# w_out's first 512 channels by Strassen's seven products, with sums taken in the accumulator banks

## The chip, the cores and the metric

The kernel runs on one core of a Trainium2 chip. Its time is the device time of one execution in microseconds (us). The engines named are TensorE (PE; PEld is its weight load), VectorE (DVE), ScalarE (ACT), GpSimd (POOL) and SyncE (SP, which issues the loads of weights).

## The reference

A decoder layer in float32 on 256 tokens with 1024 channels: a half-weighted SwiGLU layer, two parallel mixers (a Mamba-2 scan and differential attention), whose results are merged by gates and projected, and a second half-weighted SwiGLU layer, each inside RMS norms. What matters here is the middle of it:

```python
gates = jax.nn.sigmoid(gate_logits + gate_b[l]).reshape(b, L, N_BRANCH, D_MODEL)
merged = gates[:, :, 0] * y_ssd + gates[:, :, 1] * y_att
h = h + rmsnorm(merged @ w_out[l], mix_post_g[l])
h = h + 0.5 * rmsnorm(swiglu(rmsnorm(h, ffn2_pre_g[l]), ffn2_w_gate[l], ffn2_w_up[l], ffn2_w_down[l]),
                      ffn2_post_g[l])
```

`merged` is 256x1024, `w_out` 1024x1024.

## The kernel before

**Precision.** Every large product is done in three terms. A float32 operand is split into a high part (a cast on ScalarE, line 259 for weights) and a low part (raw minus high on VectorE, line 260); the terms are high x high, low x high and high x low. One matmul takes a slice of 128 channels, 128 tokens and 512 columns. So w_out takes 8 slices x 2 token blocks x 2 column halves x 3 terms = 96 matmuls.

**Weights.** SyncE loads chunks of 1 MB into three buffers (`raw`). `take` hands out the next unit of weights and, with `split_to`, has units split ahead of their use: each unit takes two casts `whi` and two subtractions `wlo` of 128x1024. A chunk's buffer is loaded anew (`load_to`) as soon as its last reader is done. A chunk of w_out is 256 channels by 1024 columns.

**Order.** TensorE's instructions run in the order in which the code writes them (`own_order(PE)`); those of VectorE, ScalarE and SyncE are put in order by a scheduler from that point of the program on. On the chip each engine does its own in the order that was set.

**The stretch around the change.** `natural` computes, for a half of the 512 columns at a time, the gates' products (`pgt`), the scan's projection (`pws`) and the attention's projection (`pwd`), for two token blocks each. When `pwd` of column half q is done, `merge` multiplies and adds with the gates (lines 1613 and 1614, tiles `gt`), and `turn_merged` turns the half by transposes on TensorE (`pmg`) and splits it into `mh` and `ml` (lines 320 and 321), so that channels stand on partitions. Both blocks of half 0 are turned after the first unit of `pwd` of half 1; half 1 is turned in w_out's first two slices. Then `mm_n` (line 676) does w_out into four banks `acc_mx`, one for each token block and column half. It does block 0's two banks first, then block 1's.

**What follows block by block.** `norm_half` takes the sum of squares of a bank on ScalarE (`jp_mxp`, line 506) and multiplies the bank by the gain on VectorE (`og_mxp`, line 605). `norm_end` has GpSimd make the reciprocal root in two steps (`rp_mxp`, lines 511 and 512), and VectorE adds the product to the residual `h` (line 645, one for each half). For the next norm, block 0 is turned raw (`pu_f`, line 520, during the last matmuls of w_out) and scaled later; its gained parts are `u_f` (lines 526 and 528). Block 1 is scaled first: two squares of `h` on ScalarE (`sq_f`), two steps on GpSimd (`r_f`), `un_f` on VectorE (line 565), and only then its turn `pu_f`, which TensorE's order has after 36 matmuls `pn_f` of the feed-forward layer's first product on block 0.

**Products by sevens that exist already.** The down projections of both feed-forward layers do part of their channels by Strassen's scheme in Winograd's form. A `Quad` is two chunks (512 channels) as four quarters of 256 channels by 512 columns. Three products take a quarter as it is (1, 2 and 3), four take a sum of quarters (5, 6, 7 and 4; `sum_of`, line 122, tile `wt`). `split` (lines 130 and 136) makes high and low part of each, `wqh` and `wql`. `sums_of` (lines 737 to 740) makes the four sums of the activations, `sv`, and splits them.

Of the kernel before, what the change touches and what calls it, by code (L numbers as in the profile page):

```python
# [47 lines left out]
SSD_US = 1.55  # L48
DOWN = {"f1": "q1 p q2 p q3 ppp", "f2": "q1 p q2 p q3 ppp"}
FIRST, LAST = (1, 2, 3, 5, 7, 6, 4), (1, 6, 7, 2, 3, 5, 4)  # L50
BREAK, STOP = object(), object()


@with_exitstack
def tile_hybrid_layer(ctx: ExitStack, tc: tile.TileContext, x, ffn1_pre_g, ffn1_w_gate, ffn1_w_up,
# [37 lines left out]
    class Quad:  # L93
# [60 lines left out]
    def n_chunk(w, k0):  # L154
        chunk(w[k0:k0 + 2 * P, :].rearrange("(j p) c -> p j c", p=P), [P, 2, D])

    def quad(w, k0, products):

        n = len(units)
        for k in (k0, k0 + 2 * P):  # L160
            n_chunk(w, k)
        del units[n:]
        q = Quad(len(chunks) - 2, products)
        units.extend((q, p) for p in products)


# [427 lines left out]

    def norm_half(n, b, q, acc, pg, fold, tag, cs=slice(0, 512)):

        if q == 0:
# [7 lines left out]
        n["mul"] = nc.vector.tensor_tensor(n["og", q][:, cs], acc[:, cs], pg[:, halves[q]][:, cs], ALU.mult).ins  # L605
# [124 lines left out]
    def sums_of(g, even, odd):  # L730
# [11 lines left out]
        split(more[:, 0], more[:, 1], v[:, 3])  # L742
        return ([hi[:, i] for i in range(3)] + [more[:, 0]], [lo[:, i] for i in range(3)] + [more[:, 1]])

    def mm_quads(acts, sums, tag):


# [10 lines left out]
        for n, (kind, j) in enumerate(of_quads):  # L758
            last = n == n_quads - 1
            if kind == "p":  # L760
                wh, wl = take()
                for kt in range(2):
                    ah, al = acts[2 * j + kt]
                    for b in range(2):
                        ts = slice(b * P, (b + 1) * P)
                        for x_, w_ in ((ah, wh), (al, wh), (ah, wl)):
                            for q in range(2):
                                p = ((2, 3), (4, 8))[b][q]
                                mm(p, x_[:, ts], w_(kt)[:, halves[q]], False)
                continue  # L770
            sh, sl = sums[j]
            for p in LAST if last else FIRST:
                wh, wl = take()
                for kt in range(2):
                    if p in (1, 2, 4):
                        k, b = {1: (0, 0), 2: (2, 0), 4: (2, 1)}[p]
                        ah, al = (x_[:, b * P:(b + 1) * P] for x_ in acts[4 * j + k + kt])
                    else:
                        ah, al = (x_[{5: 0, 6: 1, 7: 2, 3: 3}[p]][:, kt, :] for x_ in (sh, sl))
# [762 lines left out]

    own_order(PE)

    def natural(name, n, hi, lo, evict, us, then=lambda: None):


        accs = [pj(f"{name}{b}") for b in range(2)]
        for i in range(n):
            w = take()  # L1550
            for b in range(2):
                bs = slice(b * P, (b + 1) * P)
                mm_nat(accs[b], w, (lambda k: hi(k)[:, bs], lambda k: lo(k)[:, bs]), i * 4, i == 0, i == n - 1, "u")
# [14 lines left out]
    for half in range(2):  # L1568
        gb = k4([P, D], f"gb{half}")
        nc.gpsimd.dma_start(gb, gate_b[0][half * D:(half + 1) * D].partition_broadcast(P))  # L1570
        for b in range(2):
            gt[half][b] = k4([P, D], f"gt{half}{b}")
        for q in range(2):
            def gate(b, acc):
                nc.vector.tensor_tensor(gt[half][b][:, halves[q]], acc, gb[:, halves[q]], ALU.add)

            natural(f"pgt{half}{q}", 2, uh, ul, gate, GATE_US)
    opens.append(open_gates)
# [1 line left out]
        back.run(0.1)  # L1580
    for q in range(2):
        def gated(b, acc):
            t = gt[0][b][:, halves[q]]
# [6 lines left out]
    mg, merges = [], []  # L1590

    def turn_merged(n):

        for q, b, t, mh, ml in merges[:n]:
            pt = bg([P, 4, P], f"pmg{q}{b}")
            for m in range(4):
                nc.tensor.transpose(pt[:, m, :], t[:, m * P:(m + 1) * P], ident)
            bs = slice(b * P, (b + 1) * P)
            split(mh[:, :, bs], ml[:, :, bs], pt)
        del merges[:n]  # L1600

    def attended():
        back.drain()
        act_table(SILU)

    for q in range(2):
        mh = k4([P, 4, T], f"mh{q}", F32R)
        ml = k4([P, 4, T], f"ml{q}", F32R)
        mg += [(mh[:, m, :], ml[:, m, :]) for m in range(4)]

        def merge(b, acc):
            t0, t1 = gt[0][b][:, halves[q]], gt[1][b][:, halves[q]]
            nc.vector.tensor_tensor(t1, acc, t1, ALU.mult)
            nc.vector.tensor_tensor(t1, t1, t0, ALU.add)
            merges.append((q, b, t1, mh, ml))

        natural(f"pwd{q}", 2, lambda j: oh[j // 4][:, j % 4, :], lambda j: ol[j // 4][:, j % 4, :], merge,
                SSD_US if q == 0 else 0.0, (attended, lambda: turn_merged(2))[q])

    pg = load_gain(mix_post_g, "pg_mx")  # L1620
    acc = [[bg([P, 512], f"acc_mx{b}{q}") for q in range(2)] for b in range(2)]

    made, ready, turned = next_norm("f2", "f2")

    def mixed(b):
        n = {}
        for q in range(2):
            norm_half(n, b, q, acc[b][q], pg, 1.0, "mxp")
        norm_end(n, b, 1.0, "mxp")
        ready(b)  # L1630

    mm_n(acc, mg, mixed, turned, lambda: turn_merged(1))


    norm = made[0]
# [36 lines left out]
```

## Time and profile before

| | |
|---|---|
| median of 3 runs | 730.2 us (729.93 to 730.43) |
| the profiled execution's own time | 730.82 us |
| its span, first to last instruction | 728.9 us |
| granted TensorE clock over the span | 0.998 |
| issues of loads of w_out, 1 MB each | 4, 5.0 us to landing |
| POOL busy in the span | 30.6 us |

The busy time of an engine is the time in which one of its instructions runs; "idle before" and "<-" name how long an engine stood idle and what ended that. In a timeline each row has its start and its length in us from the span's start, and xN counts equal instructions that follow each other. A matmul's row is longer than the distance to the next, since matmuls overlap.

### The profile page before, as it was taken

To read this page: it belongs to the slowest core of one execution; us is meant where nothing else is said; L and a number is where in the kernel's file an instruction comes from. 1 tells how busy PE (TensorE), PEld (TensorE's weight loads), DVE (VectorE), ACT (ScalarE), POOL (GpSimd) and SP (SyncE) were. 2 spreads that over 40 slices of the span, in tenths; PEclk is the share of its full clock that TensorE was granted. 3 is DMA by queue.
4 is the path that set the end of the run, shared out by engine and by line. 5 is a ranking of instruction groups with operands and counts; after the bars stand their busy time and mean duration, and the time that the engine had idled before them with its cause. 6 is when DMAs were issued, how large, how long until landed. Compare 5 with 4: busy or idle time off the path is not lost.

```text
span 728.9 us, 10569 instructions
## 1 busy us (share of the span) xinstructions
PE 720.9 (99%) x4025; PEld 620.7 (85%) x4025; DVE 609.1 (84%) x933; ACT 472.3 (65%) x804; POOL 30.6 (4%) x63
## 2 busy tenths in 40 slices
PE   9999999999999999999999999999999999999996
PEld 7889888888878889999888788888888888888885
DVE  6978788999979999777996998785784878789996
ACT  5666566656867676869965577772563757566562
POOL 4300000000200000000000000000010000000000
PEclk9999999999999999999999999999999999999999
DMA  8874645567663657666564664465361655654551
GB/s 296 237 253 155 226 153 195 174 223 268 189 224 118 188 160 238 215 182 205 158 223 146 213 215 142 146 239 195 121 233 51 232 182 166 231 194 154 178 197 58
DMA packets 94450, 137.92 MB, mean 189 GB/s; under 512 B 2668, under 2 KB 68800, under 8 KB 94400
## 3 DMA queue, kind: packets, MB, share of 16 engines
q1 hardware_dynamic: 91728, 129.51, 53.4%
q0 software_dynamic: 2368, 7.22, 3.3%
q8 instruction: 31, 0.51, 0.3%
q10 hardware_dynamic: 304, 0.53, 0.2%
q14 instruction: 19, 0.16, 0.1%
HBM read 136.17 MB, written 1.08 MB: 188 GB/s over the span
## 4 chain that ended last, share of the span: by engine, by line
PE 96%; ACT 2%; DMA 1%; DVE 0%; issue 0%; SPq 0%; DVEq 0%; ACTq 0%
PE pup_f L341 14%; PE pg_f L341 14%; PE pxs L341 6%; PE pws L382 6%; PE pgt L382 6%; PE acc_f2p L755 5%; PE acc_f1p L755 5%; PE pbc L341 3%; PE pk L341 3%; PE pq L341 3%; PE acc_mx L676 3%; PE pn_mx L382 3%; PE pn_f L382 3%; PE pwd L382 3%; PE pn_f L398 3%; PE acc_f1p L676 2%
## 5 line engine op out<-in xcount | busy, mean ns | idle before, releaser
L260 DVE TENSOR_TENSOR wlo<-raw,whi 128x1024 fp32r<-128x1024 f32 x216 | 257.5, 1222 | 19.4 <-ACT whi L259 18.4
L259 ACT CAST whi<-raw 128x1024 fp32r<-128x1024 f32 x216 | 218.2, 1048 | 16.7 <-DMA raw<-in_w_in_dram 4.4
L341 PE MATMUL pg_f<-u_f,whi 128*128 128x512 f32 x288 | 69.0, 390 | 0.0
L341 PE MATMUL pup_f<-u_f,whi 128*128 128x512 f32 x288 | 68.7, 391 | 0.0
L341 PEld LDWEIGHTS pg_f<-u_f,whi 128*128 128x128 f32 x288 | 53.9, 188 | 11.1
L341 PEld LDWEIGHTS pup_f<-u_f,whi 128*128 128x128 f32 x288 | 52.9, 188 | 10.2
L130 ACT CAST wqh<-wt 128x1024 fp32r<-128x1024 f32 x24 | 25.2, 1054 | 23.3 <-DVE wt L122 21.9
L341 PEld LDWEIGHTS pg_f<-u_f,wlo 128*128 128x128 f32 x288 | 36.9, 191 | 1.4
L341 PE MATMUL pup_f<-u_f,wlo 128*128 128x256 f32 x288 | 37.5, 283 | 0.0
L341 PE MATMUL pg_f<-u_f,wlo 128*128 128x256 f32 x288 | 37.4, 283 | 0.0
L347 ACT COPY su_f<-pup_f 128x256 f32<-128x256 f32 x36 | 13.2, 373 | 35.7 <-PE pup_f L341 35.6
L341 PEld LDWEIGHTS pup_f<-u_f,wlo 128*128 128x128 f32 x288 | 35.9, 192 | 0.0
L348 DVE TENSOR_TENSOR su_f<-pup_f,su_f 128x256 f32<-128x256 f32 x36 | 15.3, 424 | 23.8 <-ACT su_f L347 23.7
L382 PE MATMUL pgt<-whi,u_mx 128*128 128x512 f32 x128 | 33.1, 393 | 0.0
L331 PE MATMUL pz<-u_mx,whi 128*128 128x256 f32 x128 | 31.6, 284 | 0.0
L330 PE MATMUL pz<-u_mx,whi 128*128 128x256 f32 x128 | 31.6, 284 | 0.0
L341 PE MATMUL pxs<-u_mx,whi 128*128 128x512 f32 x128 | 29.9, 390 | 0.0
L136 DVE TENSOR_TENSOR wql<-wt,wqh 128x1024 fp32r<-128x1024 f32 x24 | 29.1, 1221 | 0.2
L382 PEld LDWEIGHTS pgt<-whi,u_mx 128*128 128x128 f32 x128 | 23.6, 188 | 5.3 <-issue 0.7
L341 PEld LDWEIGHTS pxs<-u_mx,whi 128*128 128x128 f32 x128 | 23.8, 188 | 4.8
L320 ACT CAST gh_f<-sg_f 128x512 fp32r<-128x512 f32 x18 | 11.2, 620 | 23.2 <-DVE sg_f L911 20.2
L331 PEld LDWEIGHTS pz<-u_mx,whi 128*128 128x128 f32 x128 | 24.5, 192 | 0.2 <-issue 0.2
(415 smaller groups left out, 1579.5 us busy)
## 6 DMA issues: line engine op xcount, KB each, us to landing
raw<-in_w_in_dram SPq DMA_DIRECT2D x40, 1024.0 KB, 5.2
raw<-in_ffn_w_down_dram SPq DMA_DIRECT2D x22, 1024.0 KB, 4.8
raw<-in_ffn_w_gate_dram SPq DMA_DIRECT2D x20, 1024.0 KB, 5.2
raw<-in_ffn_w_up_dram SPq DMA_DIRECT2D x20, 1024.0 KB, 5.2
raw<-in_ssd_w_branch_dram SPq DMA_DIRECT2D x8, 1024.0 KB, 4.9
acb<-acd POOLq DMA_DIRECT2D x8, 512.0 KB, 4.4
raw<-in_da_w_branch_dram SPq DMA_DIRECT2D x4, 1024.0 KB, 5.5
raw<-in_w_out_dram SPq DMA_DIRECT2D x4, 1024.0 KB, 5.0
```

The lines of the kernel that those rows point to most:

```text
L130: nc.scalar.copy(hi, src)
L136: nc.vector.tensor_sub(lo, src, hi.bitcast(F32))
L259: last_cast[0] = behind(nc.scalar.copy(hi, r[:, js, :]), "cast").ins
L260: m = nc.vector.tensor_sub(lo, r[:, js, :], hi.bitcast(F32))
L330: nc.tensor.matmul(acc[m], wh(j)[:, cs], ah(k0 + j), start=first and j == ks[0], stop=False)
L331: nc.tensor.matmul(acc[m], wh(j)[:, cs], al(k0 + j), start=False, stop=False)
L341: nc.tensor.matmul(to, w_(j)[:, m * P:(m + 1) * P], x_(j), start=first and j == 0, stop=not first and j == KD - 1, skip_group_check=True)
L348: nc.vector.tensor_tensor(dst, acc[:, :T], dst, ALU.add)
L382: nc.tensor.matmul(acc, a(k0 + j), b(j), start=first and i == 0, stop=last and i == 11)
L398: nc.tensor.matmul(accs[b], x_(k0 + j), w_(j), start=first and j == 0 and w_ is wh and x_ is acts[b][0], stop=last and j == 3 and w_ is wl)
L676: nc.tensor.matmul(acc[b][q][:, cs] if to is None else to, x_[:, ts], w_(kt)[:, halves[q]][:, cs], start=to is not None and kt == 0 and x_ ...
L755: nc.tensor.matmul(bank[p], x_, w_, start=p not in begun, stop=last and p in (1, 5, 6, 7))
```

## The change

The first 512 channels of w_out become a `Quad` with products in the order 1, 2, 6, 5, 3, 7, 4, the other 512 stay plain chunks. The new `mm_mixed` takes the place of `mm_n`. With P1 to P7 the products, the four banks are made thus: bank a takes P1, is copied by ScalarE (`p1`), takes P6 on top, is copied (`u2`), takes P7 on top, is added to P5 by VectorE (`c4`), and takes P4 and the plain channels on top: this is block 1, first column half. Bank b is P2 with the plain channels, and VectorE adds `p1`: block 0, first half. Bank d is P5, copied (`p5`), then P3 and the plain channels on top, and VectorE adds `u2`: block 0, second half. Bank e is the plain channels alone, and VectorE adds `c4`: block 1, second half.

The sums of weights get no `k4` buffers but the two halves of one `u8` tile (`wt_mx`), reused for 7 and 4. Product 4's unit stands behind the two plain chunks. The gate tiles `gt` are kept by column half instead of by token block. The two turns of merged half 0 come after the first token block and after the second token block of `pwd`'s first unit (`turn_block`), with ScalarE copies of the turned tiles (`mt`) for `sums_of`; how far units are split ahead there is set by `ahead`. Half 1 is turned after products 6 and 5. A bank's norm follows its own addition (`half_mixed`).

```diff
+MIXED = (1, 2, 6, 5, 3, 7, 4)
...
-                t = k4([P, 2, 512], f"wt{self.i}{p}")
+                t = self.homes(p) if self.homes else k4([P, 2, 512], f"wt{self.i}{p}")
                 nc.vector.tensor_sub(t, self.quarter(n, p), m)
...
-    for c in range(4):
+    sums_home = []
+
+    def mixed_home(p):
+
+        if not sums_home:
+            sums_home.append(sb.tile([P, 4, 2, T], F32, tag="u8", name="wt_mx", bufs=2))
+        return sums_home[0].rearrange("p (a b) c t -> p a b (c t)", a=2)[:, {5: 0, 6: 1, 7: 0, 4: 1}[p]]
+
+    quad(w_out[0], 0, MIXED, mixed_home)
+    last_unit_mx = units.pop()
+    for c in range(2, 4):
         n_chunk(w_out[0], c * 2 * P)
+    units.append(last_unit_mx)
...
+    def mm_mixed(acts, sums, turn_next, half, done, turned):
+
+
+        at = {1: "a", 6: "a", 7: "a", 4: "a", 2: "b", 5: "d", 3: "d"}
+        banks = {"a": pj("acc_mxa")}
...
+        def piece(p, w):
+            o, (wh, wl) = at[p], w
+            if o not in banks:
+                banks[o] = bg([P, 512], f"acc_mx{o}")
+            for kt in range(2):
+                ah, al = of_piece(p, kt, acts[:4], sh, sl)
+                for x_, w_ in ((ah, wh), (al, wh), (ah, wl)):
+                    mm(o, x_, w_(kt), kt == 1 and w_ is wl and p in (1, 5, 6, 7))
+
+        def plain(b, q, i):
+            o, (wh, wl) = (("b", "d"), ("a", "e"))[b][q], ws[i]
+            for kt in range(2):
+                ah, al = (x_[:, b * P:(b + 1) * P] for x_ in acts[4 + 2 * i + kt])
+                for x_, w_ in ((ah, wh), (al, wh), (ah, wl)):
+                    mm(o, x_, w_(kt)[:, halves[q]], i == 1 and kt == 1 and w_ is wl)
+
+        piece(1, take(0))
+        nc.scalar.copy(p1, banks["a"])
+        piece(2, take(0))
+        piece(6, take(0))
+        nc.scalar.copy(u2, banks["a"])
+        turn_next()
+        piece(5, take(0))
+        nc.scalar.copy(p5, banks["d"])
+        turn_next()
+        w3, w7 = take(0), take(0)
+        ws = [take(1) for _ in range(2)]
+        plain(0, 0, 0)
+        piece(3, w3)
+        split_to(taken[0] + 1)
+        w4 = take(0)
+        plain(0, 1, 0)
+        plain(0, 0, 1)
+        half(0, 0, banks["b"], p1)
+        steps = split_steps()
+        next(steps)
+        plain(0, 1, 1)
+        half(0, 1, banks["d"], u2)
+        normed["lo"] = done(0)
+        for _ in steps:
+            pass
+        split_to(ahead_of(taken[0], AHEAD - 1))
+        piece(7, w7)
+        nc.vector.tensor_tensor(c4, banks["a"], p5, ALU.add)
+        banks["e"] = pj("acc_mxe")
+        plain(1, 1, 0)
+        plain(1, 1, 1)
+        half(1, 1, banks["e"], c4)
+        turned()
+        piece(4, w4)
+        for i in range(2):
+            plain(1, 0, i)
+        half(1, 0, banks["a"], None)
+        split_to(ahead_of(taken[0], AHEAD))
+        done(1)
...
+            if q == 0:
+                for i, x_ in enumerate(plain_mg):
+                    nc.scalar.copy(x_[:, :, bs], pt[:, 2 * i:2 * i + 2, :])
             split(mh[:, :, bs], ml[:, :, bs], pt)
...
+    def turn_block(i):
+        if i == 0:
+            turn_merged(1)
+            if not merges:
+                sums_mg.append(sums_of(0, *plain_mg))
+                split_to(taken[0] + 8)
...
+    def half_mixed(b, q, acc, rest):
+        if rest is not None:
+            nc.vector.tensor_tensor(rest, acc, rest, ALU.add)
+            acc = rest
+        norm_half(norms_mx[b], b, q, acc, pg, 1.0, "mxp")
...
-    mm_n(acc, mg, mixed, turned, lambda: turn_merged(1))
+    mm_mixed(mg, sums_mg[0], lambda: turn_merged(1), half_mixed, mixed, turned)
```

The change inserts lines, so that up to `mm_mixed` every line stands 12 later: 272 is the low part of weights that stood at 260, 657 the residual of 645, 518 the square sums of 506. In the rows below, the names of weights carry the unit's number (85 to 88 are w_out's chunks, 89 to 92 the first ones of the feed-forward layer, last digit the half or the product).

VectorE where w_out's first chunks are split, during `pwd`. Before, from the first low part of w_out to the first turned half:

```order
L260 TENSOR_TENSOR wlo850_5153<-raw85_5028,whi850_5152 128x1024
L1444 SCALAR_TENSOR_TENSOR o8_5048<-pto2_5043,g8_2085,o8_5048 128x2x256
L1584 TENSOR_TENSOR gt01_4123<-pws11_4844,gt01_4123 128x512
L1444 SCALAR_TENSOR_TENSOR o8_5048<-pto3_5064,g8_2085,o8_5048 128x2x256
L260 TENSOR_TENSOR wlo851_5157<-raw85_5028,whi851_5156 128x1024
L1613 TENSOR_TENSOR gt10_4350<-pwd00_5073,gt10_4350 128x512
```

And now, from the second of the sums of weights:

```order
L123 TENSOR_TENSOR wt_mx_5156<-raw86_5081,wt_mx_5156 128x1024
L137 TENSOR_TENSOR wql852_5159<-raw86_5081,wqh852_5154 128x1024
L137 TENSOR_TENSOR wql856_5163<-wt_mx_5156,wqh856_5161 128x1024
L137 TENSOR_TENSOR wql855_5167<-wt_mx_5156,wqh855_5165 128x1024
L123 TENSOR_TENSOR wt_mx_5156<-raw86_5081,wt_mx_5156 128x1024
L123 TENSOR_TENSOR wt_mx_5156<-raw86_5081,raw85_5028 128x1024
L1709 TENSOR_TENSOR gt10_4350<-pwd00_5071,gt10_4350 128x512
L137 TENSOR_TENSOR wql853_5173<-raw86_5081,wqh853_5169 128x1024
L1710 TENSOR_TENSOR gt10_4350<-gt10_4350,gt00_4122 128x512
```

All sums of weights and most low parts of the products stand ahead of the merges or between them, where one low part stood.

VectorE from block 0's residual to block 1's `un_f`. Before:

```order
L645 SCALAR_TENSOR_TENSOR h_72<-og_mxp01_5345,rp_mxp0_5347,h_72 128x512
L605 TENSOR_TENSOR og_mxp10_5457<-acc_mx10_5242,pg_mx_5238 128x512
L528 SCALAR_TENSOR_TENSOR u0_f2_5352<-pu_f200_5392,cols_a_112,u0_f2_5352 128x128 x4
L528 SCALAR_TENSOR_TENSOR u1_f2_5353<-pu_f201_5405,cols_a_112,u1_f2_5353 128x128 x4
L260 TENSOR_TENSOR wlo920_5483<-raw92_5362,whi920_5482 128x1024
L260 TENSOR_TENSOR wlo921_5487<-raw92_5362,whi921_5486 128x1024
L605 TENSOR_TENSOR og_mxp11_5461<-acc_mx11_5243,pg_mx_5238 128x512
L645 SCALAR_TENSOR_TENSOR h_72<-og_mxp10_5457,rp_mxp1_5463,h_72 128x512
L645 SCALAR_TENSOR_TENSOR h_72<-og_mxp11_5461,rp_mxp1_5463,h_72 128x512
L565 TENSOR_SCALAR un_f210_5476<-h_72,r_f21_5473 128x512
```

Now, in two pieces that follow each other; first from block 0's residual to the gained parts:

```order
L657 SCALAR_TENSOR_TENSOR h_72<-og_mxp01_5386,rp_mxp0_5388,h_72 128x512
L272 TENSOR_TENSOR wlo891_5396<-raw89_5177,whi891_5395 128x1024
L272 TENSOR_TENSOR wlo900_5402<-raw90_5247,whi900_5401 128x1024
L272 TENSOR_TENSOR wlo901_5406<-raw90_5247,whi901_5405 128x1024
L1726 TENSOR_TENSOR c4_mx_5283<-acc_mxe_5418,c4_mx_5283 128x512
L540 SCALAR_TENSOR_TENSOR u0_f2_5393<-pu_f200_5437,cols_a_112,u0_f2_5393 128x128
L617 TENSOR_TENSOR og_mxp11_5435<-c4_mx_5283,pg_mx_5277 128x512
L540 SCALAR_TENSOR_TENSOR u0_f2_5393<-pu_f200_5437,cols_a_112,u0_f2_5393 128x128 x3
L540 SCALAR_TENSOR_TENSOR u1_f2_5394<-pu_f201_5450,cols_a_112,u1_f2_5394 128x128 x4
```

and then to `un_f`:

```order
L272 TENSOR_TENSOR wlo910_5494<-raw91_5337,whi910_5493 128x1024
L617 TENSOR_TENSOR og_mxp10_5491<-acc_mxa_5279,pg_mx_5277 128x512
L272 TENSOR_TENSOR wlo911_5498<-raw91_5337,whi911_5497 128x1024
L657 SCALAR_TENSOR_TENSOR h_72<-og_mxp10_5491,rp_mxp1_5503,h_72 128x512
L657 SCALAR_TENSOR_TENSOR h_72<-og_mxp11_5435,rp_mxp1_5503,h_72 128x512
L272 TENSOR_TENSOR wlo920_5523<-raw92_5399,whi920_5522 128x1024
L272 TENSOR_TENSOR wlo921_5527<-raw92_5399,whi921_5526 128x1024
L577 TENSOR_SCALAR un_f210_5516<-h_72,r_f21_5513 128x512
```

Seven low parts of weights and the addition `c4` stand there, where two low parts stood; two of the seven are now between `h` and `un_f`.

ScalarE at the same place. Before:

```order
L506 ACTIVATE jp_mxp10_5455,sp_mxp1_5454<-acc_mx10_5242 128x512
L526 ACTIVATE u0_f2_5352<-pu_f200_5392,cols_a_112 128x128 x4
L526 ACTIVATE u1_f2_5353<-pu_f201_5405,cols_a_112 128x128 x4
L259 CAST whi920_5482<-raw92_5362 128x1024
L259 CAST whi921_5486<-raw92_5362 128x1024
L506 ACTIVATE jp_mxp11_5459,sp_mxp1_5454<-acc_mx11_5243 128x512
L506 ACTIVATE sq_f210_5469,ss_f21_5468<-h_72 128x512
L506 ACTIVATE sq_f211_5471,ss_f21_5468<-h_72 128x512
```

Now:

```order
L271 CAST whi910_5493<-raw91_5337 128x1024
L518 ACTIVATE jp_mxp11_5433,sp_mxp1_5432<-c4_mx_5283 128x512
L518 ACTIVATE sq_f200_5464,ss_f20_5463<-h_72 128x512
L518 ACTIVATE sq_f201_5466,ss_f20_5463<-h_72 128x512
L518 ACTIVATE jp_mxp10_5489,sp_mxp1_5432<-acc_mxa_5279 128x512
L271 CAST whi911_5497<-raw91_5337 128x1024
L271 CAST whi920_5522<-raw92_5399 128x1024
L518 ACTIVATE sq_f210_5509,ss_f21_5508<-h_72 128x512
L271 CAST whi921_5526<-raw92_5399 128x1024
L518 ACTIVATE sq_f211_5511,ss_f21_5508<-h_72 128x512
```

Block 0's squares of `h` moved behind the square sum of bank e, casts of coming weights in front of block 1's squares, and one between the two.

More of the change, by code (lines that the diff above doesn't have):

```diff
@@ L774, in mm_quads @@
                 for kt in range(2):
[L775 to L779, printed above, removed]
+                    ah, al = of_piece(p, kt, acts[4 * j:4 * j + 4], sh, sl)
                     for x_, w_ in ((ah, wh), (al, wh), (ah, wl)):
@@ L1543, in tile_hybrid_layer, with natural @@
     own_order(PE)
-    def natural(name, n, hi, lo, evict, us, then=lambda: None):
+    def natural(name, n, hi, lo, evict, us, then=lambda: None, ahead={}, behind_block=lambda i: None):
         accs = [pj(f"{name}{b}") for b in range(2)]
         for i in range(n):
-            w = take()
+            w = take(2 if i in ahead else AHEAD)
+            split_to(taken[0] + ahead.get(i, 0))
             for b in range(2):
@@ L1570, in tile_hybrid_layer @@
         nc.gpsimd.dma_start(gb, gate_b[0][half * D:(half + 1) * D].partition_broadcast(P))
-        for b in range(2):
-            gt[half][b] = k4([P, D], f"gt{half}{b}")
         for q in range(2):
+            gt[half][q] = k4([P, 2, 512], f"gt{half}{q}")
             def gate(b, acc):
-                nc.vector.tensor_tensor(gt[half][b][:, halves[q]], acc, gb[:, halves[q]], ALU.add)
+                nc.vector.tensor_tensor(gt[half][q][:, b, :], acc, gb[:, halves[q]], ALU.add)
             natural(f"pgt{half}{q}", 2, uh, ul, gate, GATE_US)
```

52 lines of the change are left out of this document (33 added, 19 removed).

## The prediction

> **What bounds the kernel now.** The first page is read for the span and the busy shares, then the waits of TensorE, then the timeline around w_out.
>
> ```profile
> span 728.9 us, 10569 instructions
> PE 720.9 (99%) x4025; PEld 620.7 (85%) x4025; DVE 609.1 (84%) x933; ACT 472.3 (65%) x804; POOL 30.6 (4%) x63
> PE 96%; ACT 2%; DMA 1%; DVE 0%; issue 0%; SPq 0%; DVEq 0%; ACTq 0%
> PE warm L475 <- DVE zeros L455: 1.1, 1, 1.1
> PE pu_f L957 <- DMA h<-in_x_dram: 0.7, 1, 0.7
> ```
>
> TensorE is busy 99% of the span, holds 96% of the chain that ended last, and has two waits in the whole program, both in the first microseconds. So a matmul less anywhere is time, as long as no wait takes its place. Whether one does is read from the engines that serve w_out. The next rows cut the stretch from the second branch projection to the turn of the next norm's second token block into three (columns: PE, PEld, DVE, ACT and POOL busy, granted clock, DMA).
>
> ```profile
> 496.50:519.30 22.80, 22.80 (x108) 18.96 (x107) 10.55 (x14) 5.56 (x8) 0.53 (x1) 1.00 0.24 75
> 519.30:543.00 23.70, 23.70 (x114) 19.68 (x113) 20.17 (x29) 16.06 (x30) 2.11 (x4) 1.00 0.77 265
> 543.00:551.10 8.10, 8.10 (x37) 6.65 (x36) 4.56 (x7) 2.77 (x7) 2.89 (x5) 1.00 0.41 129
> ```
>
> TensorE has no hole there, at a granted clock of 1.00. VectorE has 12.3 us free ahead of w_out, but only 3.5 us during it.
>
> **What is removed.** Half of w_out (four of its eight slices of 128 channels) takes 48 of the 96 matmuls of 128x512. Seven products of two slices and three terms take 42. Six fall away; transposes stay at 16 for the merged halves and 8 for each turn of the next norm.
>
> ```profile
> 519.29 0.61 PE L676 MATMUL acc_mx<-whi,mh 128*128 128x512 f32 x2
> 537.95 1.03 PE L520 MATMUL pu_f<-ident,h 128*128 128x128 f32 x8
> 542.94 1.07 PE L382 MATMUL pn_f<-whi,u_f 128*128 128x512 f32 x4
> 544.75 1.98 PE L382 MATMUL pn_f<-whi,u_f 128*128 128x512 f32 x8
> 546.57 1.07 PE L382 MATMUL pn_f<-wlo,u_f 128*128 128x512 f32 x4
> 551.11 1.03 PE L520 MATMUL pu_f<-ident,un_f 128*128 128x128 f32 x8
> ```
>
> Eight matmuls go from 544.75 to 546.57: 0.227 us each. Six are **-1.36 us**, on the path.
>
> **What is added, all off TensorE.** Prices stand in the feed-forward layers, which already do this.
>
> ```profile
> L136 DVE TENSOR_TENSOR wql<-wt,wqh 128x1024 fp32r<-128x1024 f32 x24 | 29.1, 1221 | 0.2
> L321 DVE TENSOR_TENSOR sl<-sv,sh x2: 951/952/954, 58.8 to 81.0; 128x768 fp32r<-128x768 f32 x2
> L737 DVE TENSOR_TENSOR sv<-sg_f,sg_f x2: 426/426/426, 55.9 to 78.1; 128x256 f32<-128x256 f32 x2
> L931 DVE TENSOR_TENSOR c_f<-acc_f1p,c_f x1: 679/679/679, 189.5 to 189.5; 128x512 f32<-128x512 f32 x1
> 528.23 3.49 DVE L260 TENSOR_TENSOR wlo<-raw,whi 128x1024 fp32r<-128x1024 f32 x3
> 531.64 0.69 DVE L605 TENSOR_TENSOR og_mxp<-acc_mx,pg_mx 128x512 f32<-128x512 f32 x1
> ```
>
> Three wide subtractions go from 528.23 to 531.64, so one fills 1.14 us; a row runs 0.08 us into the next, so a 128x512 one of 0.69 fills 0.61 and a 128x256 one of 0.43 fills 0.34. VectorE gets four weight sums and three more low parts (seven instead of four): 7 x 1.14 = 8.0; the sums of the activations, 4 x 0.34 + 0.87 + 0.34 = 2.6; four additions of products, 2.4. That is 13.0 us. The 12.3 us free ahead of w_out takes most of the weights, but what is queued behind comes later: by the order, when block 0's residual is written, seven low parts of coming weights still stand ahead of `un_f`, where two stood before. This is the wait to price.
>
> **The path to the second turn.** TensorE's marks follow from before's by the saving, because the same 18 matmuls stand behind the first turn `pu_f` in both, and 36 between the first `pn_f` and the second turn: first turn 537.95 - 1.36 = 536.59, second 551.11 - 1.36 = 549.75. Block 0's last bank ends 18 x 0.227 ahead of the first turn, and a matmul's result comes 0.16 behind its slot (four in 1.07 are 3 x 0.227 + 0.39): 532.66. The other engines' rows:
>
> ```profile
> 536.22 1.41 DVE L645 SCALAR_TENSOR_TENSOR h<-og_mxp,rp_mxp,h 128x512 f32<-128x512 f32 x2 [0.27 <-POOL rp_mxp L512]
> 540.09 2.16 DVE L528 SCALAR_TENSOR_TENSOR u_f<-pu_f,cols_a,u_f 128x128 fp32r<-128x128 f32 x8 [0.34 <-ACT u_f L526]
> 542.17 2.35 DVE L260 TENSOR_TENSOR wlo<-raw,whi 128x1024 fp32r<-128x1024 f32 x2
> 544.44 0.68 DVE L605 TENSOR_TENSOR og_mxp<-acc_mx,pg_mx 128x512 f32<-128x512 f32 x1
> 545.36 1.42 DVE L645 SCALAR_TENSOR_TENSOR h<-og_mxp,rp_mxp,h 128x512 f32<-128x512 f32 x2 [0.24 <-POOL rp_mxp L512]
> 548.67 1.02 DVE L565 TENSOR_SCALAR un_f<-h,r_f 128x512 f32<-128x512 f32 x2 [1.89 <-POOL r_f L512]
> 526.46 2.95 ACT L259 CAST whi<-raw 128x1024 fp32r<-128x1024 f32 x3
> 543.20 0.60 ACT L506 ACTIVATE jp_mxp<-acc_mx 128x512 f32<-128x512 f32 x1 [0.22 <-PE acc_mx L676]
> 546.21 0.63 ACT L506 ACTIVATE sq_f<-h 128x512 f32<-128x512 f32 x1 [2.32 <-DVE h L645]
> 546.87 0.63 ACT L506 ACTIVATE sq_f<-h 128x512 f32<-128x512 f32 x1
> 547.41 0.19 ACT L506 ACTIVATION_READ_ACCUMULATOR sq_f<-h 128x1 f32 x1
> 543.99 0.70 POOL L511 TENSOR_SCALAR rp_mxp<-sp_mxp 128x1 f32<-128x1 f32 x1 [4.49 <-ACT jp_mxp L506]
> 544.77 0.56 POOL L512 TENSOR_TENSOR rp_mxp<-rp_mxp,small 128x1 f32<-128x1 f32 x1
> 547.69 0.30 POOL L511 TENSOR_SCALAR r_f<-ss_f 128x1 f32<-128x1 f32 x1 [2.36 <-ACT sq_f L506]
> 548.08 0.56 POOL L512 TENSOR_TENSOR r_f<-r_f,small 128x1 f32<-128x1 f32 x1
> ```
>
> In before, `un_f`'s first half is done near 549.3, so the second turn at 551.11 has 1.8 us to spare. Now step by step, with GpSimd's first step at its two measured prices, 0.30 and 0.70, as the ends:
>
> 1. New addition u2 (0.69), then the square sum (0.60 + 0.19), from 532.66: 534.2.
> 2. GpSimd's two steps, 0.30 or 0.70, then 0.09 and 0.56, with 0.04 of handover at each change of engine: 535.2 to 535.6. The two `h` of block 0: VectorE free at 536.5 to 536.9. The first turn at 536.59 takes the halves one after the other, the second 0.4 later: a wait of 0 to 0.1.
> 3. Three low parts (3.41) and the addition of bank e to `c4` (0.61): 540.5 to 540.9.
> 4. Eight low parts of `u_f` (2.08, 540.09 to 542.17), two `og` (1.22), two low parts of weights (2.27) stand ahead of block 1's `h`: 546.1 to 546.5. In before it began at 545.36.
> 5. First `h` (0.75); square (0.66 to the next); then ScalarE does `whi921`, which the order puts between the two squares (0.95, a third of 526.46's row); second square with its readout (0.73, 546.87 to 547.60): 549.2 to 549.6, handovers included.
> 6. GpSimd 0.95 or 1.35, `un_f` 0.60, two handovers: the second turn can begin at 550.9 to 551.7 instead of 549.75.
>
> So TensorE waits 1.2 to 2.0 us; its second half adds 0.1, since `un_f`'s two halves (1.02 together) follow by some 0.5 and four transposes by 0.4. I take the middle, 1.7 in all with the 0.1, plus 0.1 at the first turn: **+1.8 us**. Behind the second turn stand this product's last 12 matmuls and all of the feed-forward layer, so the wait is lost in full; the engines that serve these were ready in before at the same distance behind the turn and move with it. Ends of the sum: -1.36 + 1.3 = -0.1 and -1.36 + 2.2 = +0.8; if GpSimd's second step is stretched too (0.40, the most that a row shows for the first), +1.2. Below: nothing excludes that ScalarE and VectorE swap waits for slack elsewhere, down to the full -1.36.
>
> For the choice between 0.30 and 0.70 the trace itself speaks: 0.70 is the row beside which VectorE ran the low parts of 542.17 (until 544.52), 0.30 the row at which VectorE stood still. In the new order `wlo921` runs at the last 0.30-or-0.70 step and an `og` with one PSUM operand at the first, so 0.70 is nearer at the end, 0.30 at the start; the middle holds both. [...]
>
> **Sum.** -1.36 + 1.8 = +0.45 us. The profiled execution took 730.82 (span 728.9), so it would be 731.3; it lies 0.6 above the shown median of 730.2, which goes to **730.7 us**.
>
> What hides the rest: weight sums ride on VectorE's 12.3 free us; ScalarE's copies out of the banks (0.60 each) sit ahead of products that reuse the bank only after six other matmuls (1.36). Loads: the buffer of the last chunk before the second `pn_f` comes free when `wlo891` ends (537.7 to 538.1).
>
> ```profile
> raw<-in_ffn_w_up_dram SPq DMA_DIRECT2D x20, 1024.0 KB, 5.2
> 507.51 1.07 PE L382 MATMUL pwd<-whi,oh 128*128 128x512 f32 x4
> ```
>
> With 5.2 us it lands at 543.3; ScalarE asks for it near 544.8. No new wait.
>
> **Rivals.** (a) *The saving comes whole*: 730.2 - 1.36 = 728.8. For it: in before this turn had 1.8 us in hand, and a chain that ends 1.7 us sooner than in my sum would not be seen. Against: seven wide low parts stand in one queue. Chance 0.10.
> (b) *VectorE becomes the bound ahead of w_out.* The first projection block of the second half begins at 507.51; the second transposes come 24 matmuls and 4 transposes later, 513.4, their copies end near 514.3. From there VectorE has sums (2.6), one low part of the merge (0.61), two wide low parts (2.28) and the second half's four merge steps (2.44): 7.9, done at 522.2. TensorE turns that half 18 matmuls into w_out, 519.29 + 4.09 = 523.4. Spare: 1.2 us. If VectorE is later than that, each microsecond more is TensorE's here, and stays late until `un_f`: 2.5 us late gives +0.45 + 1.3 = +1.8, 732.0. For it: 13 us of new work in a stretch where 15.8 are free. Against: prices measured in the same shapes. Chance 0.14, deciding from 1.2 us of lateness; slower beyond what can be told from 2.2 us on.
> (c) *Something else holds the queue of ScalarE or the loads*: 731 to 733, chance 0.04.
> The forecast has 0.72, its own range 730.1 to 731.4.
>
> **Numbers.** A measurement of this kernel tells 0.2% (1.46 us) from no change: below 728.74 is faster, above 731.66 slower. Rival (a) sits at the edge, mostly inside: faster 0.04. Slower: most of (b) and (c), 0.15, and 0.06 of the forecast's tail: 0.21. Within: 0.75. The range 729.3 to 732.0 leaves out most of (a) and the ends of (b) and (c).
>
> **What would show it.** In the changed profile: 90 matmuls of 128x512 for w_out; a wait of `pu_f` on VectorE's `un_f` of 1.2 to 2.1 us, the only large one; VectorE without a hole from block 0's `h` to block 1's; a `whi` cast between the two squares; no wait of the `pmg` transposes. I am wrong if `un_f` is done before 549.75 on this clock, or if `pmg` or the first products wait.

## The result and the profile after

| | before | changed |
|---|---|---|
| median of 10 runs each | 730.48 us (729.93 to 731.45) | 732.56 us (731.62 to 734.56) |
| ratio to before, 95% interval | | 1.003 (1.0019 to 1.0040) |
| the profiled execution: time, span | 730.82, 728.9 us | 733.45, 731.7 us |
| 128x512 matmuls of w_out | 96 | 90 |

The kernel became 2.1 us slower; 730.7 was predicted, with 732.0 as the upper end. The page of the changed kernel, its waits of TensorE (us in total, times, longest), and two stretches of the table by windows (columns as in the prediction: PE, PEld, DVE, ACT, POOL, granted clock, DMA):

```profile
span 731.7 us, 10595 instructions
PE 721.6 (99%) x4019; PEld 621.0 (85%) x4019; DVE 621.3 (85%) x950; ACT 479.1 (65%) x816; POOL 33.1 (5%) x63
PE pu_f L532 <- DVE un_f L577: 2.6, 1, 2.6
PE warm L487 <- DVE zeros L467: 1.1, 1, 1.1
PE pn_mx L394 <- DVE wlo L272: 0.4, 1, 0.4
541.48:549.80 8.32, 8.32 (x37) 6.57 (x35) 7.47 (x15) 5.61 (x12) 3.94 (x4) 1.00 0.73 245
549.80:555.78 5.98, 3.39 (x14) 3.08 (x13) 3.11 (x8) 3.12 (x11) 2.04 (x3) 0.71 0.75 239
```

Six matmuls fewer are there (4025 to 4019), and the wait is where the prediction put it, but 2.6 us long. (The wait of `pn_mx` lies at 195 to 200 us, far ahead of the change, and comes and goes: the second profile of the same kernel, below, has none.) The second thing stands in the last row: from 549.80 the granted clock is 0.71 over the stretch, where before had 1.00 from 496.50 to 551.10. The timeline of TensorE shows what that is:

```profile
552.39 1.94 PE L532 MATMUL pu_f<-ident,un_f 128*128 128x128 f32 x8 [2.59 <-DVE un_f L577]
553.99 1.95 PE L394 MATMUL pn_f<-whi,u_f 128*128 128x512 f32 x4
555.78 1.08 PE L394 MATMUL pn_f<-wlo,u_f 128*128 128x512 f32 x4
```

From 552.39 to 553.99 eight transposes take 1.60 us, and four matmuls 1.79; the same rows of before take 0.79 (551.11 to 551.90) and 1.00. TensorE works at half rate for 3.39 us after the wait (the granted clock from 552.39 to 555.78 is 0.51), and loses 1.6 us: 0.81 on the transposes, 0.79 on the matmuls. The span agrees: -1.36 (six matmuls) + 2.6 (wait) + 1.6 (half rate) = +2.8, and it went from 728.9 to 731.7.

Now the chain that ends in `un_f`, in order of time, from the timelines of VectorE, ScalarE and GpSimd:

```profile
535.24 1.42 DVE L657 SCALAR_TENSOR_TENSOR h<-og_mxp,rp_mxp,h 128x512 f32<-128x512 f32 x2 [0.56 <-POOL rp_mxp L524]
...
541.38 0.61 ACT L518 ACTIVATE sq_f<-h 128x512 f32<-128x512 f32 x1
...
542.61 0.58 ACT L518 ACTIVATE jp_mxp<-acc_mxa 128x512 f32<-128x512 f32 x1
...
542.80 0.31 POOL L523 TENSOR_SCALAR r_f<-ss_f 128x1 f32<-128x1 f32 x1 [7.60 <-ACT sq_f L518]
543.19 1.69 POOL L524 TENSOR_TENSOR r_f<-r_f,small 128x1 f32<-128x1 f32 x1
543.24 1.22 DVE L272 TENSOR_TENSOR wlo<-raw,whi 128x1024 fp32r<-128x1024 f32 x1
544.97 1.39 POOL L523 TENSOR_SCALAR rp_mxp<-sp_mxp 128x1 f32<-128x1 f32 x1
544.98 1.22 DVE L272 TENSOR_TENSOR wlo<-raw,whi 128x1024 fp32r<-128x1024 f32 x1
546.45 0.56 POOL L524 TENSOR_TENSOR rp_mxp<-rp_mxp,small 128x1 f32<-128x1 f32 x1
547.04 1.41 DVE L657 SCALAR_TENSOR_TENSOR h<-og_mxp,rp_mxp,h 128x512 f32<-128x512 f32 x2 [0.85 <-POOL rp_mxp L524]
548.37 2.44 DVE L272 TENSOR_TENSOR wlo<-raw,whi 128x1024 fp32r<-128x1024 f32 x2
548.51 1.03 ACT L271 CAST whi<-raw 128x1024 fp32r<-128x1024 f32 x1
550.27 0.71 POOL L523 TENSOR_SCALAR r_f<-ss_f 128x1 f32<-128x1 f32 x1 [3.26 <-ACT sq_f L518]
551.65 1.02 DVE L577 TENSOR_SCALAR un_f<-h,r_f 128x512 f32<-128x512 f32 x2 [0.84 <-POOL r_f L524]
```

The first `r_f` (542.80) is that of block 0. In before GpSimd did it four microseconds earlier. From the timeline of before:

```profile
538.55 0.31 POOL L511 TENSOR_SCALAR r_f<-ss_f 128x1 f32<-128x1 f32 x1 [2.36 <-ACT sq_f L506]
```

Block 1's `rp_mxp` followed there only at 543.99. Now ScalarE's order has block 0's squares `sq_f` at 541.38, so `r_f` comes just ahead of block 1's `rp_mxp` in GpSimd's queue. A step that takes 0.56 us elsewhere took 1.69, and the next 1.39 instead of 0.30: they end 0.42 and 0.16 us after the `wlo` of VectorE that began within 0.05 us of them (543.24 + 1.22, 544.98 + 1.22). Such a step is called held below. VectorE, whose queue has come to block 1's `h`, stands still for 0.85 us until `rp_mxp` is there.

By the clock the times fall into two groups. Here are the 10 executions above with the 5 of a second set (`after_again`, below), by the mean granted clock that each recorded:

| granted clock | executions | us | mean |
|---|---|---|---|
| 0.999 | 7 | 731.63, 732.01, 732.71, 731.95, 731.62, 732.40, 731.52 | 731.98 |
| 0.996 or 0.997 | 8 | 733.45, 732.85, 734.56, 733.91, 733.56, 734.72, 733.20, 733.78 | 733.75 |

3.39 us at half rate lower the mean over 730 us by 0.0023, about the difference of the two groups in the clock, and the mean times lie 1.8 us apart, about the 1.6 that a half-rate stretch costs. The profiled execution is of the second group. A mean of 0.997 alone proves nothing: 12 of the 75 executions of the kernel before that stand beside the experiments have it too, at 730.12 to 732.89 us, 0.3 above the others on the mean. Here clock and time go together.

### The profile page after: what moved, and what is told of

Same layout as the page of the kernel before. It is cut to its first block, busy times and chain, and to the rows that moved or that the text cites. A ratio compares the mean times of both kernels' runs of the same rounds, so it can differ in the third digit from the quotient of the medians.

```text
span 731.7 us, 10595 instructions
## 1 busy us (share of the span) xinstructions
PE 721.6 (99%) x4019; PEld 621.0 (85%) x4019; DVE 621.3 (85%) x950; ACT 479.1 (65%) x816; POOL 33.1 (5%) x63
## 4 chain that ended last, share of the span: by engine, by line
PE 86%; DVE 6%; ACT 3%; issue 2%; DMA 1%; POOL 1%; DVEq 0%; ACTq 0%; POOLq 0%
PE pup_f L353 14%; PE pg_f L353 14%; PE pxs L353 6%; PE pws L394 6%; PE pgt L394 6%; PE acc_f2p L843 5%; PE pbc L353 3%; PE pk L353 3%; PE pq L353 3%; PE pn_f L410 3%; PE pwd L394 3%; PE pn_mx L394 2%; PE acc_f2p L688 2%; PE pn_f L394 2%; DVE wlo L272 2%
## 5 line engine op out<-in xcount | busy, mean ns | idle before, releaser
L272 DVE TENSOR_TENSOR wlo<-raw,whi 128x1024 fp32r<-128x1024 f32 x212 | 252.6, 1219 | 18.9 <-ACT whi L271 18.3
L271 ACT CAST whi<-raw 128x1024 fp32r<-128x1024 f32 x212 | 214.4, 1048 | 13.8 <-DMA raw<-in_w_in_dram 5.5
L137 DVE TENSOR_TENSOR wql<-raw,wqh 128x1024 fp32r<-128x1024 f32 x21 | 25.4, 1219 | 3.6 <-ACT wqh L131 3.6
```

The lines of the kernel that those rows point to most:

```text
L137: nc.vector.tensor_sub(lo, src, hi.bitcast(F32))
L271: last_cast[0] = behind(nc.scalar.copy(hi, r[:, js, :]), "cast").ins
L272: m = nc.vector.tensor_sub(lo, r[:, js, :], hi.bitcast(F32))
```

## The experiments

Two theories had to be told apart from what else a crowded stretch could do. **A**: the wait is long because GpSimd's one-column steps, two of them for block 0, lie on block 1's path and are held beside VectorE's low parts. **B**: the rest of the loss is TensorE's half rate after an idle wait, and comes in some executions only. Every ratio below is to the kernel before, measured beside the experiment.

**1. Other low parts** (`one_input`).

```diff
-            m = nc.vector.tensor_sub(lo, r[:, js, :], hi.bitcast(F32))
+            if i in (91, 92):
+                m = nc.vector.tensor_scalar(lo, r[:, js, :], hi[:, 0, 0:1].bitcast(F32), None, ALU.mult)
+            else:
+                m = nc.vector.tensor_sub(lo, r[:, js, :], hi.bitcast(F32))
```

> The four low parts ahead of un_f (wlo910, wlo911, wlo920, wlo921) are made by an instruction with one wide SBUF input (raw times a number) in place of raw minus high, in the same place and order and nearly as long (un_f of 128x512 fills 0.5 us, so about 1.0 instead of 1.2 us each); the subtraction of these four is left out. Theory A (GpSimd's one-column steps are held by VectorE's instructions with two SBUF inputs): r_f of block 0 and rp_mxp of block 1 fall from 1.69 and 1.39 us to 0.56 and 0.30, block 1's h starts near 546.0 instead of 547.04, the turn waits 0.7 to 1.1 us instead of 2.6 and no half-rate stretch follows: 1.6 us off the wait alone, up to 3.2 with the half rate, so 729.5 to 731.0 against 732.56 before the edit. Rival (VectorE's queue as such is late, whatever its instructions read): the steps stay near 1.4 to 1.7 us or the wait shrinks only by the 4 x 0.2 us of shorter low parts, 731.8 to 732.5.

Measured: 730.48 us, ratio 0.9996 (0.9987 to 1.0005). Its timeline:

```profile
542.35 1.22 POOL L527 TENSOR_TENSOR r_f<-r_f,small 128x1 f32<-128x1 f32 x1
542.40 0.75 DVE L273 TENSOR_SCALAR wlo<-raw,whi 128x1024 fp32r<-128x1024 f32 x1
543.66 0.91 POOL L526 TENSOR_SCALAR rp_mxp<-sp_mxp 128x1 f32<-128x1 f32 x1
543.66 0.75 DVE L273 TENSOR_SCALAR wlo<-raw,whi 128x1024 fp32r<-128x1024 f32 x1
550.20 1.06 PE L535 MATMUL pu_f<-ident,un_f 128*128 128x128 f32 x8 [1.24 <-DVE un_f L580]
```

The time is as theory A had it, for a reason it did not have; the wait, 1.24 us, is a little above the 0.7 to 1.1 that it gave. GpSimd's steps are still held, at 1.22 and 0.91: again they end 0.42 and 0.16 us after the VectorE instruction beside them. That instruction is only shorter (0.75 us for 128x1024, where 1.0 was expected), and so is the hold; VectorE's queue is shorter by as much, so this run does not tell the two apart. A second wide SBUF input, which the expectation took for the condition, is not needed for a hold, then: these instructions read one wide operand, and the steps beside them took 1.22 and 0.91 us, against 0.56 and 0.30 where VectorE stood still. What makes an instruction hold a step, no run here shows.

**2. Block 0's norm behind block 1's** (`r0_late`), and **3. GpSimd's part of that alone** (`pool_late`, where ScalarE's squares stay).

```diff
-            self.r0 = rms(0, self.tag)
+            if self.tag == "mx":
+                self.r0 = rms(0, self.tag)
...
             unit_done["lo"] = last_unit[0]
+            if not scalar:
+                self.r0 = rms(0, self.tag)
```

In `pool_late` the two squares are issued where they were, and only `rstd_of` stands behind, with a dependence on block 1's last step.

> Block 0's squares and reciprocal root for the next norm (sq_f, r_f), which the feed-forward layer needs only at its settle step, go behind block 1's on ScalarE and GpSimd. Theory A: GpSimd starts block 1's rp_mxp near 542.6 instead of 544.97, its second step is the one that runs into wlo910 or the like, block 1's h starts near 546.2 instead of 547.04 (VectorE's queue is then what holds it), the last r_f is still held beside wlo921; the turn waits 1.2 to 2.1 us instead of 2.6: 730.7 to 732.0 against 732.56. Rival (ScalarE and GpSimd order does not matter, the low parts on VectorE set the wait): wait 2.5 to 2.7, 732.4 to 732.7.

> Only GpSimd's two steps for block 0's r_f go behind block 1's; ScalarE's squares and everything else stay in their order. The squares of block 0 then still hold jp_mxp of acc_mxa back until 543.1. If the two held GpSimd steps of r_f ahead of rp_mxp made the wait: rp_mxp starts near 543.2, is done by 545.2 to 545.4, h starts when VectorE's queue lets it (546.1 to 546.3), the turn waits 1.5 to 1.9 us without a half-rate stretch, 730.6 to 731.2. If the order of the squares on ScalarE made it: rp_mxp is held beside both low parts, h starts at 546.9 or later, the turn waits 2.3 us or more, 732.0 to 732.6.

Measured: `r0_late` 730.77 us, ratio 1.0000 (0.9991 to 1.0009); `pool_late` 730.96 us, ratio 1.0007 (0.9998 to 1.0015). Timeline of `r0_late`:

```profile
541.20 1.90 DVE L540 SCALAR_TENSOR_TENSOR u_f<-pu_f,cols_a,u_f 128x128 fp32r<-128x128 f32 x7
542.30 0.31 POOL L523 TENSOR_SCALAR rp_mxp<-sp_mxp 128x1 f32<-128x1 f32 x1 [7.33 <-ACT jp_mxp L518]
542.69 0.56 POOL L524 TENSOR_TENSOR rp_mxp<-rp_mxp,small 128x1 f32<-128x1 f32 x1
545.88 1.41 DVE L657 SCALAR_TENSOR_TENSOR h<-og_mxp,rp_mxp,h 128x512 f32<-128x512 f32 x2
551.12 1.07 PE L532 MATMUL pu_f<-ident,un_f 128*128 128x128 f32 x8 [1.54 <-DVE un_f L577]
551.94 1.17 PE L394 MATMUL pn_f<-whi,u_f 128*128 128x512 f32 x4
```

Timeline of `pool_late`:

```profile
543.59 1.26 POOL L523 TENSOR_SCALAR rp_mxp<-sp_mxp 128x1 f32<-128x1 f32 x1 [8.17 <-ACT jp_mxp L518]
546.32 1.41 DVE L659 SCALAR_TENSOR_TENSOR h<-og_mxp,rp_mxp,h 128x512 f32<-128x512 f32 x2
551.56 1.06 PE L534 MATMUL pu_f<-ident,un_f 128*128 128x128 f32 x8 [1.55 <-DVE un_f L579]
```

Both waits are 1.5 us, so it is GpSimd's order, not ScalarE's, that made the wait 1.0 us longer: this part of theory A is shown. In `r0_late` block 1's two steps take 0.31 and 0.56 beside `u_f`, which VectorE reads from PSUM: not held. In `pool_late` one step is still held (1.26), but it is done before VectorE's queue gets to `h`, and `h` is no longer preceded by a hole. In both, the transposes run at full rate again (551.12 to 551.94 and 551.56 to 552.38: 0.82). Two profiles prove little here, as some executions of the changed kernel do without the half rate too; the times say more. Before's medians in the two sets (730.87 and 730.45) less 1.36 and with a wait of 1.5 give 731.0 and 730.6, and 1.6 more would be 732.6 and 732.2; of the 22 executions one (732.19, of `pool_late`) is that high.

**4. Work in the wait** (`fill12`).

```diff
...
         pu = bg([P, 4, P], f"pu_{name}{b}{q}")
+        if (b, q, name) == (1, 0, "f2"):
+            (ah, _), (wh, _) = filler
+            for i in range(12):
+                nc.tensor.matmul(pu.rearrange("p m t -> p (m t)"), ah(i % 4), wh(i % 4), start=True, stop=True)
...
```

> Twelve more matmuls of 128x512 (2.7 us of work, result overwritten) stand ahead of the second turn, so TensorE is busy through the wait and un_f comes when it came. Theory B (the idle wait makes TensorE run at half rate for some 3 us after it, 1.6 us lost): the turn starts 0.1 to 0.2 us later than in the changed kernel, the eight transposes take 0.8 us and the four matmuls 1.0 us again, 731.0 to 731.6 against 732.56, and the runs lie within 0.3%. Rival (the slow stretch belongs to the wait for un_f's second half or to the buffers, not to TensorE's rate): transposes and matmuls stay at 1.6 and 1.8 us, 732.6 to 732.9.

Measured: 731.92 us, ratio 1.0016 (1.0007 to 1.0025); 11 executions between 730.99 and 732.61.

```profile
550.13 2.88 PE L536 MATMUL pu_f<-whi,u_f 128*128 128x512 f32 x12
552.85 1.04 PE L538 MATMUL pu_f<-ident,un_f 128*128 128x128 f32 x8
553.65 1.18 PE L394 MATMUL pn_f<-whi,u_f 128*128 128x512 f32 x4
```

The turn starts when it did (in this execution all marks lie 0.46 to 0.48 us later, the held `r_f` at 543.67 instead of 543.19; the steps take 1.69 and 1.39 us here as well), but TensorE did not idle, and the transposes take 0.80 us. One profile cannot decide, as half of the changed kernel's executions have no half rate either. But the median, 731.92, lies at the mean of the first group in the table above (731.98), and there is no second group by the clock: the two executions at 0.997 took 731.37 and 732.15, none has 0.996. The median is 0.3 above the range that was expected; that range took the half rate off every execution, and it is in about half of them.

**5. The wait without the change** (`before_d14`, `before_d11`): instructions of 128x512 ahead of `un_f` in the kernel before.

```diff
         un = k2([P, 512], f"un_{tag}{b}{q}")
+        for _ in range(more):
+            eng.tensor_scalar(un, h[:, b, halves[q]], 0.5, None, ALU.mult)
...
```

`more` is 14 or 11 for the first half of `un_f` and 0 elsewhere.

> The kernel before, with 14 more VectorE instructions of 128x512 (0.43 us each, values overwritten) ahead of un_f, nothing else: un_f comes 14 x 0.43 + 0.43 - 1.89 = 4.6 us later, of which 1.8 were to spare, so the turn waits 2.8 us. Theory B: half rate after the wait, so 730.5 + 2.8 + 1.6 = 734.9 (in executions without it 733.3). Rival (a wait costs its own length, and the slow stretch belongs to the changed kernel): 733.3 in all executions.

> The kernel before with 11 instead of 14 added VectorE instructions ahead of un_f. With 14 the wait was 3.70 us and one instruction filled 0.466 us (11 in 5.12), so here the turn waits 2.3 us. If the half rate comes with a wait that long: about 730.9 + 2.3 + 1.6 = 734.8, and the transposes take 1.6 us; if it needs a longer one (2.6 us in the changed kernel had it, 1.5 us with block 0's norm behind had not): 733.2, and the transposes take 0.8 us.

Measured: `before_d14` 736.72 us (735.47 to 737.13), ratio 1.0076 (1.0063 to 1.0089); `before_d11` 734.13 us (732.52 to 735.29), ratio 1.0051 (1.0038 to 1.0064). TensorE in `before_d14`:

```profile
554.36 1.97 PE L520 MATMUL pu_f<-ident,un_f 128*128 128x128 f32 x8 [3.70 <-DVE un_f L567]
555.98 1.92 PE L382 MATMUL pn_f<-whi,u_f 128*128 128x512 f32 x4
557.74 1.10 PE L382 MATMUL pn_f<-wlo,u_f 128*128 128x512 f32 x4
```

TensorE in `before_d11`:

```profile
552.94 1.10 PE L520 MATMUL pu_f<-ident,un_f 128*128 128x128 f32 x8 [2.58 <-DVE un_f L567]
553.78 1.96 PE L382 MATMUL pn_f<-whi,u_f 128*128 128x512 f32 x4
555.54 1.90 PE L382 MATMUL pn_f<-wlo,u_f 128*128 128x512 f32 x4
557.25 2.04 PE L382 MATMUL pn_f<-whi,u_f 128*128 128x512 f32 x8
```

The waits were 0.9 and 0.3 us longer than expected: in `before_d14` an added instruction filled 0.466 us instead of 0.43, and `un_f`'s other half ran between the added ones; the rest of the miss stays open. The times bear the half rate out. All five executions of `before_d14`, expected at 734.9, lie above 730.87 + 3.70 = 734.6, the price of the wait alone, at clocks of 0.995 to 0.997. Of `before_d11`, three at 0.997 took 734.13 to 735.29 and two at 0.999 took 732.52 and 734.01. The half rate is there in the old kernel too, so it belongs to the wait and not to the seven products. In `before_d14` it starts with the turn and lasts 3.38 us; in `before_d11` the transposes run at full rate, and eight matmuls behind them take 3.47 us instead of 1.82. In the changed kernel the granted clock is 0.50 from 552.27 to 555.68, 3.41 us, begun 0.12 us ahead of the turn, and the slow rows last 3.39 us. So the three lengths lie close together, 3.38 to 3.47 us, after waits of 3.70, 2.59 and 2.58 us, while the start does not keep one distance from the wait: in `before_d11` the slow rows begin at 553.78, 0.84 us after the turn. What sets the length and the start, no run here shows.

**6. The changed kernel again** (`after_again`).

> The changed kernel once more. Theory B: executions come in two groups 1.6 us apart, near 731.9 (730.5 - 1.36 + 2.6 + 0.1) with a granted clock of 0.998 to 0.999 and near 733.5 with 0.996 to 0.997; the half rate of 3.3 us in 730 takes 0.0023 off the clock's mean. Rival (one group, spread by 0.3%): times do not go with the clock.

Measured: 733.56 us (731.52 to 734.72), ratio 1.0036 (1.0023 to 1.0050). Four executions are in the second group of the table above, one (731.52, clock 0.999) in the first, and that one was profiled. Its clock and its timeline of TensorE:

```profile
core 0: 729.8 us, clock 0.999
551.98 1.06 PE L532 MATMUL pu_f<-ident,un_f 128*128 128x128 f32 x8 [2.61 <-DVE un_f L577]
552.80 1.17 PE L394 MATMUL pn_f<-whi,u_f 128*128 128x512 f32 x4
```

The same kernel, the same wait of 2.6 us, and no half rate: transposes in 0.82 us, span 729.8 instead of 731.7. With the experiments 4 and 5, theory B is shown for a wait of this length; what decides in a single execution is not.

**7. The chain served first** (`casts_first`, `low_last`). Block 0's norm goes behind block 1's as above; unit 91's and 92's casts are issued ahead of block 1's squares, the low parts `wlo91` behind its `h` and `wlo92` behind `un_f`. `low_last` also takes the terms with the weights' low part last in the unit behind the turn.

```diff
...
         half(1, 0, banks["a"], None)
-        split_to(ahead_of(taken[0], AHEAD))
-        done(1)
+        l91, d91 = split_late()
+        l92, d92 = split_late()
+        cast_first[0] = last_cast[0]
+        h1 = done(1)
+        l91(h1)
+        d91()
+        l92(last_unit[0])
+        d92()
...
-                        mm_nat(acc, ws[2 * i + c], act, c * 4, c == 0, c == 1, "u")
+                        mm_nat(acc, ws[2 * i + c], act, c * 4, c == 0, c == 1,
+                               "w" if self.tag == "f2" and n == 3 else "u")
...
```

`split_late` makes a unit's two casts and returns its two subtractions, which take a dependence on what is given.

> The changed kernel with the chain to un_f served first: block 0's norm behind block 1's on ScalarE and GpSimd; the casts whi920 and whi921 ahead of block 1's squares; on VectorE block 1's h ahead of wlo910 and wlo911, un_f ahead of wlo920 and wlo921. If the chain is only queues, h starts near 544.0, un_f near 549.0, the turn does not wait (549.65), and four matmuls behind it wait 0.4 us for wlo920: 730.9 - 1.36 + 0.4 = 729.9. Rival (the seven products cost something that the queues do not show): 730.5 or more.

> The same, and in the one unit behind the turn (92, block 0) the terms with the low part of the weights come last in place of second, so that wlo920 is needed 0.9 us later. No wait is left behind the turn: 730.9 - 1.36 = 729.5 (729.2 to 729.8). Rival: the wait moves to the low parts of u_f for block 1, 729.9 or more.

> The fastest kernel so far once more, beside the others of this set: 729.0 (728.6 to 729.4), ratio 0.997 to 0.999, against 730.45 less 1.36 = 729.1 from the six matmuls.

Measured: `casts_first` 729.49 us, ratio 0.9983 (0.9974 to 0.9992); `low_last` 728.97 us, ratio 0.9978 (0.9969 to 0.9987), and again 728.87 us, ratio 0.9976 (0.9967 to 0.9985). The first two lie 0.4 and 0.2 us below what was expected, because 730.9 was taken for the kernel before, which stood at 730.45 in that set. Timeline of `low_last`, first measurement:

```profile
544.47 1.42 DVE L682 SCALAR_TENSOR_TENSOR h<-og_mxp,rp_mxp,h 128x512 f32<-128x512 f32 x2 [0.16 <-POOL rp_mxp L547]
549.00 0.89 DVE L602 TENSOR_SCALAR un_f<-h,r_f 128x512 f32<-128x512 f32 x2 [0.84 <-POOL r_f L547]
549.12 1.08 PE L417 MATMUL pn_f<-whi,u_f 128*128 128x512 f32 x4
550.04 1.04 PE L555 MATMUL pu_f<-ident,un_f 128*128 128x128 f32 x8
550.83 2.09 PE L417 MATMUL pn_f<-whi,u_f 128*128 128x512 f32 x8
```

`h` starts 2.6 us earlier than in the changed kernel, and the turn follows the last matmul without a wait. 730.45 - 1.36 = 729.1: within the interval, the six matmuls come whole. The wait of 0.4 us that `casts_first` was expected to keep for `wlo920` did not show. The first matmuls that use `wlo920`, from the timeline of `casts_first`, have no idle time before them:

```profile
551.34 1.11 PE L417 MATMUL pn_f<-wlo,u_f 128*128 128x512 f32 x4
```

The two versions differ by less than their intervals.

**8. The order without the products** (`before_order`): the kernel before with block 0's norm behind block 1's and the low terms of unit 92 last.

> The kernel before (no seven products) with the two edits of order that it can take: block 0's squares and reciprocal root behind block 1's, and the low terms of unit 92 last. TensorE did not wait there, so if the gain of the kernel with the chain served first is the six matmuls, nothing changes: 730.2 to 730.8, ratio 0.9995 to 1.0005. Rival (the order alone gains, the seven products nothing): 729.0 to 729.6.

Measured: 730.25 us, ratio 0.9994 (0.9985 to 1.0003), no change that can be told. So the gain of `low_last` is not one of these two edits of order by themselves; the moved casts and low parts were not tried in the kernel before, where the turn did not wait either.

## Why the prediction was wrong, point by point

- **The saving.** -1.36 us was right, in the count of matmuls and, within the interval, in `low_last`'s time.
- **Steps 1 to 3** held: `h` of block 0 starts at 535.24, predicted 535.2 to 535.6; the first turn did not wait.
- **Step 4 failed.** It has block 1's `h` begin when VectorE's queue gets to it, 546.1 to 546.5. VectorE was there by 546.2, so its queue was priced rightly, but `rp_mxp` was not: `h` began at 547.04, after a hole of 0.85 us where the prediction's signs had none. The step left out block 0's `r_f`, which the new order sets right ahead of `rp_mxp` on GpSimd, and GpSimd's steps were priced at 0.30 to 0.70 where they took 1.69 and 1.39 beside whole low parts. A low part beside GpSimd was weighed for the last step only, where 0.71 was measured; at `rp_mxp` the prediction put an `og` beside it (beside which a step of before took 0.56, at 544.77, as it does alone, at 548.08), and it was `wlo911`. And the most that the trace of before happened to show was taken as the most that a step can take. That row of 0.70 was itself a held step that began late in a low part: 543.99 + 0.70 = 544.69 is 0.17 us after the end of `wlo` at 544.52. With the two block-0 steps out of the way (`pool_late`) `h` begins at 546.32 and the wait is 1.55 us, both inside the ranges of the sum. The time is 0.5 us above before's, beside the +0.45 that was forecast; the interval is 1.2 us wide, and `r0_late`, with the same wait, lies 0.1 below before's.
- **Steps 5 and 6** passed on what step 4 gave them: `whi921` between the squares, 0.71 and 0.56 on GpSimd. The turn came at 552.39, past the upper end of 551.7.
- **"So TensorE waits 1.2 to 2.0 us"** failed in kind as well: the sum takes a wait at its length. At 2.6 us it was followed by half rate in 8 of 15 executions, going by their clocks and times, at 1.6 to 1.8 us each, some 0.9 on the mean. No term of the sum and no rival had it.
- Together: +0.45, +0.8 for the longer wait (2.6 against 1.8) and 0.9 for the half rate make +2.2; +2.1 was measured.
- **Rival (a)**, the saving whole, did not happen here; it is what the kernel gives once the chain is served first. **Rival (b)** is refuted, though its price of 732.0 came close: the list of waits has no `pmg` and no first product. Its own sum held: VectorE was through the second half's merge at 522.39, predicted 522.2. **Rival (c)** named ScalarE's queue or the loads; it was GpSimd's.

## What to carry to other kernels

When a change reorders a stretch, follow every engine's queue on the path, the almost idle ones too, and ask which instruction that nobody waits for yet now stands ahead of one that is waited for. Price a small GpSimd step by the VectorE instruction that may run beside it, not by its own duration: here 0.56 and 0.30 us became 1.69 and 1.39. And count a wait of TensorE as long as those here, 2.58 to 3.70 us, as more than its length: in 8 of 15 executions of the changed kernel, going by their clocks and times, what followed it ran at half rate, at 1.6 to 1.8 us each.

## What the runs showed of the hardware

- A one-column GpSimd step that began beside a low part of weights (all operands in SBUF) ended 0.16 to 0.18 us (TENSOR_SCALAR) or 0.42 us (TENSOR_TENSOR) after it: 1.39, 0.91 and 1.26, or 1.69 and 1.22 us, where the steps take 0.30 and 0.56 alone. So it was held for what was left of that instruction. Beside `u_f`, which reads PSUM, the two steps took 0.31 and 0.56 (`r0_late`).
- After waits of 2.58 us (`before_d11`), 2.59 us (the changed kernel) and 3.70 us (`before_d14`) TensorE had rows at about half rate for 3.47, 3.39 and 3.38 us in the profiled executions; after 2.61 us in another execution of the changed kernel (`after_again`), and after 1.24, 1.54 and 1.55 us (`one_input`, `r0_late`, `pool_late`), it had none. No wait between 1.55 and 2.58 us was tried.
